# Distance-16 scores copied by ScalarE, and seven places for the raw operands of the down products

## The chip, the cores and the metric

The kernel runs on one core of one Trainium2 chip. The core has TensorE (PE, matmuls; its weight loads are shown as PEld), VectorE (DVE), ScalarE (ACT), GpSimd (POOL) and SyncE (SP), which here issues every DMA. The metric is the device time of one execution in microseconds, the median of three runs.

## What is computed

One step of a one-layer streaming encoder, on a prompt of 1024 frames and a running stream of 32 frames, all in float32, with D_MODEL 1024 and D_FF 2816:

```python
def run_trunk(x, states, params):          # DEPTH = 1
    ...
    h, st_new = mixer(rms_norm(x, g_mix_pre[l]), st, ...)
    x = x + rms_norm(h, g_mix_post[l])
    h, ffn_buf = conv_ffn(rms_norm(x, g_ffn_pre[l]), states[6][l], ...)
    x = x + rms_norm(h, g_ffn_post[l])

def conv_ffn(xn, buf, w_up, conv_w, conv_b, w_down):
    up = xn @ w_up
    up, buf = causal_dwconv(up, buf, conv_w, conv_b)
    gate, val = jnp.split(up, 2, axis=-1)
    return (jax.nn.gelu(gate, approximate=True) * val) @ w_down, buf

def gated_linear_scan(q, k, v, log_a, s0, L):     # in chunks of L = 64 (32 for the stream)
    def step(s, inp):
        ...
        diff = b[:, :, None] - b[:, None, :]
        decay = jnp.where(mask, jnp.exp(jnp.where(mask, diff, 0.0)), 0.0)
        scores = jnp.einsum('bihd,bjhd,bijhd->bijh', qc, kc, decay)
        o = (jnp.einsum('bijh,bjhv->bihv', scores, vc)
             + jnp.einsum('bihk,bhkv->bihv', qc * jnp.exp(b), s))
        ...
```

The mixer projects its input, runs three groups of heads (two gated linear scans of 6 and 5 heads, and 5 mLSTM heads), norms and gates them, and projects back.

## The kernel before

**Products in two halves.** Float32 operands are split into a rounded high half and the rest: ACT casts (line 95), DVE subtracts (line 98), and each product becomes three matmuls (lines 89 to 91).

**Units and levels.** Tokens are worked in units of 128 (u = 0 to 7, each two chunks of 64) and one of 32 (u = 8). Inside a chunk the decays between two positions are built by distance: `level` makes, for c = 32, 16, 8, 4, 2, 1, the scores between the first and the second half of every block of 2c positions, into a PSUM tile sc that has one buffer and takes two levels at a time. `copy_scores` places them in the score matrix P. The first level is copied by ACT as plain rectangles; all others go through `put`, a DVE copy under a mask (line 808). The mixers of one group of units run among the in-projections of the next.

**Up and down.** The up projection is computed in a Strassen form with seven products (tiles pux, puw, puy, puz) over 22 steps f. The down projection has two parts. The units 0, 8 and 4 take a plain product (tiles pd, into eight PSUM banks) over f, whose transposed rows of h are loaded into hr (two buffers of 288 columns). The other six units take seven products p1, p2, p6, p5, p3, p7, p4 (function `seven`), each a sum over k = 0 to 10. For one k, 384 columns of rows (h_d, or sums in s_d) and 512 columns of weights (w_dn, or sums in t_d) are loaded into one raw tile, here named rp, whose pool tag y0 has three buffers. `h_halves` makes hhp and hlp from the rows (two buffers each for odd and for even k), `weight_halves` makes wdp (seven buffers), and three PSUM banks (pdx, pdy or pdw) take three matmuls each. When a product is done, its banks are copied or added to others, and finished units are normed and stored. The tags y0 (3), y1 (1), st (1) and bw (2) are those of the up projection's results; down there only y0 is used again.

**Order.** The order of instructions on each engine is planned before compilation: `play` is a list scheduler over the whole program that keeps a queue for each engine, prices each instruction (`PRODUCT` for the matmuls by columns, a queue model for the DMAs) and takes the ready one with the longest tail. Every engine then works strictly in that order. A DMA's consumers become ready in the plan at `stop`.

Of the kernel before, what the change touches and what calls it, by code (L numbers as in the profile page):

```python
# [9 lines left out]
F32 = mybir.dt.float32  # L10
# [21 lines left out]
NCOL = 2 * HW  # L32
# [9 lines left out]
def fcol(u):  # L42

    return 128 * u if u < 4 else SMP if u == 8 else GAP_P + 2 + 128 * (u - 4)
# [35 lines left out]
def body(ctx: ExitStack, tc: tile.TileContext, a: dict):  # L80
    nc = tc.nc
    act, dve, pool, pe, sp = nc.scalar, nc.vector, nc.gpsimd, nc.tensor, nc.sync
# [588 lines left out]
    def mixer(u, g, ci0):  # L671
        n = 128 if u < 8 else DEC
# [130 lines left out]
        def put(c, src):  # L803
            mk_ = masks[:n, lev_index[c]:lev_index[c] + 1, :cl]
            dst = P[:n, :, :cl]
            if c:
                mk_, dst, src = second(mk_, c), second(dst, c), src.rearrange("p h (b c) -> p h b c", c=c)
            dve.copy_predicated(dst, mk_.broadcast_to([n, 11, *mk_.shape[2:]]), src)  # L808
# [39 lines left out]
        def copy_scores(c, sc, lv):  # L848
            s = sc[:, :, 32 * lv:32 * lv + cl // 2]
            if c == levels[0]:  # L850
                for (o, m) in chunks:
                    act.copy(P[o:o + c, :, c:2 * c], s[o:o + c])
            else:
                put(c, s[:n])

# [15 lines left out]
        for lv, c in enumerate(pairs[0]):  # L871
            copy_scores(c, sc, lv)
# [38 lines left out]
        for lv, c in enumerate(pairs[1]):  # L911
            copy_scores(c, sc, lv)
# [72 lines left out]
    P = mx.tile([128, 11, 64], F32, name="P")  # L985
# [319 lines left out]
    def down_all(ph, p6, gp):  # L1305
        xres = {}

        def wide(name):
            return p6.tile([128, 1024], F32, tag="wide", name=name, bufs=4)
# [33 lines left out]
        def h_halves(name, w, r, pool_, tag):  # L1343
            hh, hl = (pool_.tile([128, 384], F32R, tag=f"{tag}{x}", name=f"h{x}{name}", bufs=2) for x in "hl")
            split(hh[:, :w], hl[:, :w], r, dve)
            return hh, hl


        off, w = {}, 0
        for u in FIRST:  # L1350
            off[u] = w
# [2 lines left out]
        banks = [p.tile([128, 512], F32, tag=t, name=f"pd0_{i}", bufs=b) for i, (p, t, b) in enumerate(where)]  # L1354
        pair = []
        for f in range(NF):
            r = ph.tile([128, 288], F32, tag="hr", name=f"hr{f}", bufs=2)
            for u in FIRST:
                n = 128 if u < 8 else DEC
                sp.dma_start(r[:, off[u]:off[u] + n], h_d[f, :, fcol(u):fcol(u) + n])  # L1360
            hh, hl = h_halves(f"0_{f}", w, r, ph, "h")
            wr = praw[0].tile([128, 1024], F32, tag="raw", name=f"wd0_{f}r", bufs=2) if f < 2 else                 wide(f"wd0_{f}r")
            sp.dma_start(wr, a["w_dn"][f])
            wd = [weight_halves(f"wd0_{f}{hf}", wr[:, 512 * hf:512 * hf + 512]) for hf in range(2)]
            pair.append(wr)
            if f % 2:
                if f // 2 >= len(EARLY):
                    sums(f // 2, pair)
                pair = []
            if f == NF - 6:  # L1370
                sp.dma_start(gp, a["grows"][1:2, :].broadcast_to([128, 1024]))
                for u in FIRST:
                    residual(u)
            for d in range(8):
                c = slice(128 * (d % 4), 128 * (d % 4) + 128)
                mm3(banks[d][:, :w], [t[:, c] for t in wd[d // 4]], (hh[:, :w], hl[:, :w]), f == 0, f == NF - 1)
# [27 lines left out]
        def seven(p, ps, first):  # L1404
            ops = []
            for k in range(NP):
                r = ph.tile([128, NCOL], F32, tag="y0", name=f"r{p}_{k}", bufs=3)
                sp.dma_start(r[:, :384], ASRC[p](k))
                sp.dma_start(r[:, 384:896], BSRC[p](k))
                hh, hl = h_halves(f"{p}_{k}", 384, r[:, :384], *((ph, "h") if k % 2 else (p6, "g")))  # L1410
                wd = weight_halves(f"wd{p}_{k}", r[:, 384:896])
                ops.append((k, hh, hl, wd))
                if k == NP - 2:
                    continue
                for i in range(3):
                    c = slice(128 * i, 128 * i + 128)
                    for (j, hh, hl, wd) in ops:
                        mm3(ps[i], (hh[:, c], hl[:, c]), wd, first and j == 0, j == NP - 1, skip_group_check=True)
                ops = []
                if k % 3 == 0 and todo:  # L1420
                    todo.pop(0)()
# [173 lines left out]
AHEAD = {"mx": 10000., "psm": 10000., "pdx0": 1400., "pdx1": 700., "pdw0": 1400., "pdw1": 700., "pt": 130000.}  # L1595
ENGINES = ("PE", "DVE", "Activation", "Pool", "SP")
WINDOW = 3413.3
PRODUCT = {512: 232., 384: 175.5, 288: 133.5, 282: 131.5, 274: 126.5, 256: 118.}
PACKET = ((4, 9), (32, 9), (128, 13), (256, 18), (512, 27), (1024, 46), (1536, 65), (2048, 84), (4096, 159), (8192, 330), (1 << 16, 2640))
TABLES = {"Ln": 5, "Gelu_apprx_tanh": 11, "Exp": 0, "Tanh": 0, "Square": 0}  # L1600

# [94 lines left out]
def _product(i):  # L1696
# [9 lines left out]
    if mode == (128, 128) or (mode == (128, 32) and not f32) or mode == (32, 128):  # L1706
        g = PRODUCT.get(n, n / 2.4 + 12) if not f32 else max(n * 2 / 2.4 + 2.5, 60) if tr else 2 * max(n * 2 / 2.4 + 8, 112)
        return g, True, (128, 128) if mode == (128, 32) else mode, cells, (r, sums)
# [160 lines left out]
def play(g, tail, change, slack=None):  # L1869
# [6 lines left out]
    rows, held, seen, known, count = {}, [], [-1] * len(g.pred), dict.fromkeys(ENGINES, -1), 0  # L1876
    port, queue = {"DVE": 0., "Pool": 0.}, 0.
# [24 lines left out]
    while True:  # L1902
        t, e = min(((free[e] if ready[e] else max(free[e], at[wait[e][0][2]]), k) for k, e in enumerate(ENGINES) if ready[e] or wait[e]),
                   default=(None, None))
        if e is None:
            break
        e = ENGINES[e]
        while wait[e] and wait[e][0][0] <= t + 1e-6:
            heapq.heappush(ready[e], heapq.heappop(wait[e])[1:])
        if not ready[e]:  # L1910
            heapq.heappush(ready[e], heapq.heappop(wait[e])[1:])
        if e == "PE" and len(ready[e]) > 1:
            c = min(heapq.nsmallest(12, ready[e]), key=lambda x: x[0] + (change if mm[x[1]][2] != mode else 0))
            ready[e].remove(c)
            heapq.heapify(ready[e])
        else:
            c = heapq.heappop(ready[e])
        n = c[1]
        t = max(t, at[n])
        d, own, lock = cost[n]  # L1920
        sync = max([known[e]] + [seen[q] for q in g.pred[n] if eng[q] != "PE" or e != "PE"])
        if e == "PE" and any(k in rows and rows[k][0] != mm[n][4][0] and rows[k][1] > sync for k in mm[n][4][1]):
            held.append(c)
            continue
        if e == "SP" and queue - t - 1400 > BACKLOG:
            heapq.heappush(ready[e], c)
            free[e] = queue - 1400 - BACKLOG + 5
            continue
        if e == "Pool" and lock and port["DVE"] > t:
            heapq.heappush(ready[e], c)  # L1930
            free[e] = port["DVE"] + 5
            continue
        if e == "SP":
            free[e] = t + own
            queue = max(t + 1400, queue) + d
            stop = queue + 650
        elif e == "PE":
            d, wide, m, cl, (row, sums) = mm[n]
            if mode not in (None, m):
                t = max(t, max(cells) + (93 if mode == (128, 128) else 45))  # L1940
            mode, t = m, max([t] + [cells[c] for c in cl])
            if wide:
                free[e] = clock.run(t, d)
                cells = [free[e]] * 16
                stop = free[e] + 166
            else:
                f = clock.factor(t)
                for c in cl:
                    cells[c] = t + d * f
                clock.add(t, 14)  # L1950
                free[e] = t + 14 * f
                stop = t + d * f + 168
        else:
            if e == "DVE" and lock:
                t = max(t, port["Pool"])
                port["DVE"] = t + d
            if e == "Pool" and lock == 1:
                port["Pool"] = t + d
            if g.table[n] not in (None, table):
                table = g.table[n]  # L1960
                t += 1283
            free[e], stop = t + own, t + d
        if e == "PE":
            rows.update((k, (row, count)) for k in sums)
            seen[n], count = count, count + 1
            if sync > known[e]:
                while held:
                    heapq.heappush(ready[e], held.pop())
        else:
            seen[n] = sync  # L1970
        known[e] = sync
        start[n], end[n] = t, stop
        seq[e].append(n)
        release(n)
# [143 lines left out]
```

## Time and profile before

| | us |
|---|---|
| median of three runs (lowest to highest) | 1357.84 (1354.48 to 1359.75) |
| the profiled execution: time | 1356.24 |
| its span from the first to the last instruction | 1354.4 |
| PE busy in the span | 1303.9 |
| mean granted TensorE clock | 0.992 |

In the profile, a row of a stretch gives for each engine the busy time and, in brackets, the number of instructions, then the granted clock, the mean busy share of the 16 DMA engines and the GB/s moved. A timeline row gives the start, the duration, the engine, the line, the operation, the tiles written and read and the count; in square brackets stands how long the engine had been idle before it, and what ended that. A row of the waits gives the waiting engine and tile, what released it, the total, the times and the longest. Buffer numbers are left out of the names: wdp stands for wdp1 to wdp7, and so on.

### The profile page before, as it was taken

How to read it: one execution, taken by the hardware profiler on the slowest of the kernel's cores; microseconds unless marked ns; L12 is line 12 of the kernel's file. 1: busy time of each engine (PE TensorE's matmuls, PEld its weight loads, DVE VectorE, ACT ScalarE, POOL GpSimd, SP SyncE). 2: the span in 40 equal slices, each digit the busy share in tenths (PEclk: the TensorE clock that was granted, in tenths of full speed). 3: DMA queues.
4: the chain of work that ended last, by engine and by line, in shares of the span. 5: the costliest groups of instructions: out<-in, count | busy, mean ns of one | idle time of the engine just before them, and what ended most of it. 6: DMA issues, size and time to landing. Idle time of an engine off the chain costs nothing.

```text
span 1354.4 us, 30370 instructions
## 1 busy us (share of the span) xinstructions
PE 1303.9 (96%) x11977; PEld 1207.9 (89%) x11977; DVE 1039.2 (77%) x1884; ACT 710.6 (52%) x1400; POOL 181.9 (13%) x331
## 2 busy tenths in 40 slices
PE   6999999999999999999899999999999999998997
PEld 5999999998898887678899999999999999886775
DVE  6795549757889468878899988888888877755576
ACT  5654556545576554436754544545545454555554
POOL 2010100100102112222012211111111110000011
PEclk9999999999999999999999999999999999999998
DMA  9899869976898964635156623323223189786675
GB/s 327 260 330 332 266 243 333 301 260 203 287 305 288 331 231 121 202 95 171 69 199 230 215 97 109 102 87 119 80 87 119 71 275 290 261 265 192 218 248 205
DMA packets 148422, 285.24 MB, mean 211 GB/s; under 512 B 30039, under 2 KB 84471, under 8 KB 148279
## 3 DMA queue, kind: packets, MB, share of 16 engines
q1 hardware_dynamic: 148279, 283.30, 62.2%
q8 instruction: 94, 1.54, 0.5%
q14 instruction: 49, 0.40, 0.1%
HBM read 201.90 MB, written 81.34 MB: 209 GB/s over the span
## 4 chain that ended last, share of the span: by engine, by line
PE 69%; DMA 14%; DVE 9%; ACT 4%; issue 3%; SPq 1%; POOL 0%; DVEq 0%; ACTq 0%; POOLq 0%
PE pux L91 4%; PE pux L89 4%; PE pux L90 4%; PE pv L89 4%; PE pv L91 4%; PE pv L90 4%; DMA rp<-t_d 4%; PE pf L89 3%; PE pf L91 3%; PE pf L90 3%; PE puw L90 3%; PE puw L91 3%; PE puw L89 3%; DMA rp<-in_w_dn 2%; PE zp L89 2%
## 5 line engine op out<-in xcount | busy, mean ns | idle before, releaser
L1250 DVE SCALAR_TENSOR_TENSOR y<-uu,fconv_sb,y 128x1060 f32<-128x1060 f32 x88 | 115.8, 1320 | 7.9 <-ACT y L1248 7.4
L98 DVE TENSOR_TENSOR wdp<-rp,wdp 128x512 fp32r<-128x512 f32 x77 | 53.2, 691 | 56.2 <-ACT wdp L95 55.9
L95 ACT CAST wdp<-rp 128x512 fp32r<-128x512 f32 x77 | 47.7, 620 | 70.4 <-DMA rp<-t_d 39.0
L1248 ACT ACTIVATE y<-uu,fconv_sb 128x1060 f32<-128x1060 f32 x44 | 56.1, 1278 | 25.9 <-POOL uu L1245 21.5
L1196 ACT COPY c<-pux 128x274 f32<-128x274 f32 (+1 forms) x132 | 46.3, 381 | 33.9 <-PE pux L91 30.1
L926 POOL TENSOR_TENSOR hrs<-hss,mhalf 128x5 f32<-128x5 f32 (+3 forms) x27 | 35.8, 1330 | 175.3 <-DVE hss L925 172.6
L89 PE MATMUL pv<-wt_0h,xh 128*128 128x256 f32 (+2 forms) x195 | 53.8, 297 | 2.6 <-DVE xl L309 1.3
L91 PE MATMUL pv<-wt_0h,xl 128*128 128x256 f32 (+2 forms) x195 | 51.7, 288 | 0.0
L90 PE MATMUL pv<-wt_0l,xh 128*128 128x256 f32 (+2 forms) x195 | 51.5, 287 | 0.0
L89 PE MATMUL pdx<-wdp,hhp 128*128 128x512 f32 x132 | 44.8, 404 | 6.7 <-ACT hhp L95 4.6
L89 PE MATMUL pv<-wt_1h,xh 128*128 128x256 f32 (+2 forms) x195 | 49.1, 288 | 0.0
L91 PE MATMUL pv<-wt_1h,xl 128*128 128x256 f32 (+2 forms) x195 | 48.6, 288 | 0.0
L1245 POOL COPY uu<-fcache_sb 128x2 f32<-128x2 f32 x44 | 23.4, 531 | 186.1 <-DVE uu L1201 186.1
L90 PE MATMUL pv<-wt_1l,xh 128*128 128x256 f32 (+2 forms) x195 | 48.3, 288 | 0.0
L98 DVE TENSOR_TENSOR hlp<-rp,hhp 128x384 fp32r<-128x384 f32 x77 | 41.8, 552 | 5.4 <-ACT hhp L95 2.9
L90 PE MATMUL pdx<-wdp,hhp 128*128 128x512 f32 x132 | 43.9, 395 | 0.0
L91 PE MATMUL pdx<-wdp,hlp 128*128 128x512 f32 x132 | 42.9, 395 | 0.1
L95 ACT CAST hhp<-rp 128x384 fp32r<-128x384 f32 x77 | 38.4, 511 | 5.8 <-PE pdx L90 3.1
L89 PEld LDWEIGHTS pv<-wt_0h,xh 128*128 128x128 f32 (+1 forms) x195 | 35.2, 189 | 4.6 <-DVE xl L309 1.6
L211 POOL TENSOR_SCALAR gss<-gss 128x1 f32<-128x1 f32 (+1 forms) x9 | 7.4, 817 | 233.7 <-ACT gjk L1324 158.2
L89 PEld LDWEIGHTS pdx<-wdp,hhp 128*128 128x128 f32 x132 | 24.8, 191 | 13.9 <-ACT hhp L95 6.7
L808 DVE COPY_PREDICATED P<-masks_sb,sc 128x352 f32<-128x352 int32 (+1 forms) x44 | 29.8, 678 | 8.8 <-PE sc L773 8.3
(1781 smaller groups left out, 5144.4 us busy)
## 6 DMA issues: line engine op xcount, KB each, us to landing
h_d<-y SPq DMA_DIRECT2D x22, 530.0 KB, 5.1
rp<-t_d SPq DMA_DIRECT2D x44, 256.0 KB, 3.8
wt_0r<-in_w_tok SPq DMA_DIRECT2D x21, 512.0 KB, 5.9
wt_1r<-in_w_tok SPq DMA_DIRECT2D x21, 512.0 KB, 5.0
rp<-in_w_dn SPq DMA_DIRECT2D x33, 256.0 KB, 3.7
rp<-s_d SPq DMA_DIRECT2D x44, 192.0 KB, 3.9
wt_0l<-lt_d SPq DMA_DIRECT2D x14, 512.0 KB, 4.7
wt_1l<-lt_d SPq DMA_DIRECT2D x14, 512.0 KB, 5.8
```

The lines of the kernel that those rows point to most:

```text
L89: pe.matmul(ps, lh[0], rh[0], start=first, stop=False, **kw)
L90: pe.matmul(ps, lh[0], rh[1], start=False, stop=False, **kw)
L91: return pe.matmul(ps, lh[1], rh[0], start=False, stop=last, **kw)
L95: act.copy(hi, src)
L98: (eng or pool).tensor_tensor(lo, src, hi.bitcast(F32), op=ALU.subtract)
L211: pool.tensor_scalar(out, ss, other, EPS, op0=ALU.add, op1=ALU.add)
L808: dve.copy_predicated(dst, mk_.broadcast_to([n, 11, *mk_.shape[2:]]), src)
L926: pool.tensor_tensor(rs[:n, h0:h0 + nh], ss[:n, h0:h0 + nh], mhalf[:n, :nh], op=ALU.pow)
L1196: act.copy(t, ps)
L1245: pool.tensor_copy(u[:, GAP_S:GAP_S + 2], fcache[:, j, :])
L1248: act.activation(y, u, AF.Identity, scale=fconv[:, j, 2:3], bias=fconv[:, j, 3:4])
L1250: dve.scalar_tensor_tensor(y, uu[i][:, s:s + NCOL], fconv[:, j, s:s + 1], y, op0=ALU.mult, op1=ALU.add)
```

## The change

Three edits. The level c = 16 is copied by ACT as four rectangles of 16 partitions by 11 heads by 16 columns; in the unit of 32 that level is the first one and was copied so before. The raw tiles of the seven products rotate over seven places of the same size in the tags y0, bw, y1 and st, and every second pair of hr tiles takes a bw buffer. And numbers of the planner change: the prices of matmuls, and a load counts as landed 1250 instead of 650 ns after its packets.

```diff
             if c == levels[0]:
                 for (o, m) in chunks:
                     act.copy(P[o:o + c, :, c:2 * c], s[o:o + c])
+            elif c == 16:
+                for o in range(0, n, 32):
+                    b = o % 64
+                    act.copy(P[o:o + c, :, b + c:b + 2 * c], s[o:o + c, :, b // 2:b // 2 + c])
             else:
                 put(c, s[:n])
...
+        places = [("y0", 3), ("bw", 2), ("y0", 3), ("y1", 1), ("y0", 3), ("bw", 2), ("st", 1)]
+        count = [0]
+
+        def raw(name):
+            t, b = places[count[0] % 7]
+            count[0] += 1
+            return ph.tile([128, 896], F32, tag=t, name=name, bufs=b)
...
-            r = ph.tile([128, 288], F32, tag="hr", name=f"hr{f}", bufs=2)
+            r = ph.tile([128, 288], F32, tag="hr", name=f"hr{f}", bufs=2) if f % 4 < 2 else \
+                ph.tile([128, 288], F32, tag="bw", name=f"hr{f}", bufs=2)
...
-                r = ph.tile([128, NCOL], F32, tag="y0", name=f"r{p}_{k}", bufs=3)
+                r = raw(f"r{p}_{k}")
...
-PRODUCT = {512: 232., 384: 175.5, 288: 133.5, 282: 131.5, 274: 126.5, 256: 118.}
+PRODUCT = {512: 227.5, 384: 175., 288: 132.5, 282: 131., 274: 127., 256: 119.5}
...
         if e == "SP":
             free[e] = t + own
             queue = max(t + 1400, queue) + d
-            stop = queue + 650
+            stop = queue + 1250
```

The new numbers move instructions nearly everywhere. In the rows below, the number behind a name's k tells one tile from another.

On ACT, at the start of the product p6 before (wdp_k and hhp_k are the halves of weights and rows of step k, rp_k their raw tile):

```order
L95 CAST wdp_0_15923<-rp_0_15916 128x512
L95 CAST hhp_10_15888<-rp_10_15885 128x384
L95 CAST wdp_1_15942<-rp_1_15935 128x512
L95 CAST hhp_1_15938<-rp_1_15935 128x384
L95 CAST hhp_0_15919<-rp_0_15916 128x384
L95 CAST wdp_2_15961<-rp_2_15954 128x512
L95 CAST wdp_3_15980<-rp_3_15973 128x512
L95 CAST hhp_2_15957<-rp_2_15954 128x384
L95 CAST hhp_3_15976<-rp_3_15973 128x384
```

The casts of weights and of rows of one k follow each other closely.

At the same place now:

```order
L95 CAST wdp_0_15947<-rp_0_15940 128x512
L95 CAST hhp_9_15902<-rp_9_15899 128x384
L95 CAST wdp_1_15966<-rp_1_15959 128x512
L95 CAST hhp_10_15912<-rp_10_15909 128x384
L95 CAST wdp_2_15985<-rp_2_15978 128x512
L95 CAST hhp_1_15962<-rp_1_15959 128x384
L95 CAST wdp_3_16004<-rp_3_15997 128x512
L95 CAST hhp_0_15943<-rp_0_15940 128x384
L95 CAST wdp_4_16023<-rp_4_16016 128x512
L95 CAST hhp_3_16000<-rp_3_15997 128x384
L95 CAST wdp_5_16042<-rp_5_16035 128x512
```

The casts of weights now stand two to three k ahead of those of the rows.

On SP, in the first down product (hr are its rows, wd its weights, t_d the stored sums), p1's raw tiles before:

```order
L1236 DMA t_d<-wd_20r 128x1024
L1409 DMA rp_3_15495<-in_w_dn 128x512
L1408 DMA rp_3_15495<-h_d 128x384
L1236 DMA t_d<-wd_21r 128x1024
L1409 DMA rp_4_15537<-in_w_dn 128x512
L1408 DMA rp_4_15537<-h_d 128x384
```

The loads of k = 3 and 4 stand behind the last stores of the weights' sums.

Now they stand among the hr loads:

```order
L1422 DMA rp_2_15500<-in_w_dn 128x512
L1373 DMA hr_15028<-h_d 128x128 x2
L1373 DMA hr_15028<-h_d 128x32
L1376 DMA wd_15r<-in_w_dn 128x1024
L1421 DMA rp_2_15500<-h_d 128x384
L1422 DMA rp_4_15561<-in_w_dn 128x512
L1373 DMA hr_15074<-h_d 128x128 x2
L1373 DMA hr_15074<-h_d 128x32
L1421 DMA rp_4_15561<-h_d 128x384
L1240 DMA t_d<-wd_12r 128x1024
```

Four of them (k = 2, 3, 4 and 6) are issued before the first of those stores or soon behind it; k = 1 and 5 wait for the bw places behind the hr loads.

On ACT, at the scores of the third unit now (vth are gates, wt weights of the in-projection):

```order
L852 COPY P<-sc_0_2544 32x11x32 x2
L856 COPY P<-sc_0_2544 16x11x16
L324 CAST wt_7_0h<-wt_7_0r 128x1024
L101 ACTIVATE vth_5_4008<-pv_5_3982 128x256
L856 COPY P<-sc_0_2544 16x11x16 x2
L101 ACTIVATE vth_5_4038<-pv_5_4012 128x256
L856 COPY P<-sc_0_2544 16x11x16
```

The four new copies (line 856) stand partly behind other work of ACT; before, one masked copy stood on DVE in their place.

## The prediction

> **What bounds the kernel now.** I read the busy shares first, then the same engines in six stretches cut where the work changes, then the list of waits, and then the timeline at the places where TensorE stands still.
>
> ```profile
> PE 1303.9 (96%) x11977; PEld 1207.9 (89%) x11977; DVE 1039.2 (77%) x1884; ACT 710.6 (52%) x1400; POOL 181.9 (13%) x331
> ...
> core 0: us, PE busy (x) PEld busy (x) DVE busy (x) ACT busy (x) POOL busy (x), PEclk, DMA share, GB/s
> 0.00:200.00 200.00, 185.88 (x1471) 175.89 (x1472) 124.40 (x222) 108.88 (x194) 20.83 (x47) 1.00 0.87 296
> 200.00:640.00 440.00, 428.48 (x5599) 378.78 (x5597) 343.12 (x776) 235.89 (x522) 68.43 (x88) 0.99 0.72 239
> 640.00:1110.00 470.00, 464.56 (x3752) 462.66 (x3752) 407.23 (x609) 242.43 (x435) 79.26 (x180) 1.00 0.38 132
> 1110.00:1171.00 61.00, 58.74 (x436) 57.36 (x435) 48.82 (x83) 29.13 (x57) 0.00 (x0) 1.00 0.90 293
> 1171.00:1347.00 176.00, 166.25 (x726) 133.19 (x724) 111.89 (x192) 93.73 (x194) 11.36 (x15) 0.99 0.69 224
> ```
>
> TensorE (PE) is the bound nearly everywhere, so a change can only bring what PE waits. The idle time is stretch minus busy: 14.1 us in the first 200, 11.5 in the mixer stretch, 5.4 in the up stretch, 2.3 where the first down product runs, and 9.8 in the seven down products. The last is dense for its length (5.5% against 2.6% in the mixers), and there PE should have nothing but products. I take it apart next: these are the seven products' casts and subtracts, and who waits for what.
>
> ```profile
> L95 ACT CAST hhp<-rp x77: 494/511/526, 1110.3 to 1341.1; 128x384 fp32r<-128x384 f32 x77
> L98 DVE TENSOR_TENSOR hlp<-rp,hhp x77: 535/552/559, 1114.6 to 1341.8; 128x384 fp32r<-128x384 f32 x77
> L95 ACT CAST wdp<-rp x77: 605/621/625, 1165.1 to 1337.7; 128x512 fp32r<-128x512 f32 x77
> L98 DVE TENSOR_TENSOR wdp<-rp,wdp x77: 673/692/694, 1165.8 to 1338.3; 128x512 fp32r<-128x512 f32 x77
> ...
> DMA to landing us min/median/max: 2.9/4.0/5.6
> ...
> ACT wdp L95 <- DMA rp<-t_d: 39.0, 33, 2.1
> ACT wdp L95 <- DMA rp<-in_w_dn: 30.8, 23, 2.9
> ```
>
> The two wait rows (releaser, us in total, times, the longest) say that 56 of the 77 weight casts found their raw operand not landed and ScalarE (ACT) stood 69.8 us for it. A wait of ACT costs nothing by itself; the next rows show where it reaches PE.
>
> ```profile
> 1201.36 0.84 PE L89 MATMUL pdy<-wdp,hhp 128*128 128x512 f32 x3
> 1202.04 0.84 PE L90 MATMUL pdy<-wdp,hhp 128*128 128x512 f32 x3
> ...
> 1216.31 0.32 SPq L1409 DMA_DIRECT2D rp<-t_d  x1
> 1219.49 0.62 ACT L95 CAST wdp<-rp 128x512 fp32r<-128x512 f32 x1 [1.23 <-DMA rp<-t_d]
> 1220.75 1.02 DVE L98 TENSOR_TENSOR hlp<-rp,hhp 128x384 fp32r<-128x384 f32 x2
> 1221.33 0.32 SPq L1409 DMA_DIRECT2D rp<-t_d  x1
> 1224.64 0.62 ACT L95 CAST wdp<-rp 128x512 fp32r<-128x512 f32 x1 [1.80 <-DMA rp<-t_d]
> 1225.73 0.50 PE L89 MATMUL pdx<-wdp,hhp 128*128 128x512 f32 x1 [2.02 <-ACT hhp L95]
> ...
> 1251.61 0.74 PE L89 MATMUL pdw<-wdp,hhp 128*128 128x512 f32 x2 [1.71 <-ACT hhp L95]
> ...
> 1299.27 0.98 PE L89 MATMUL pdx<-wdp,hhp 128*128 128x512 f32 x3 [1.79 <-ACT hhp L95]
> ...
> 1319.63 0.62 ACT L95 CAST wdp<-rp 128x512 fp32r<-128x512 f32 x1 [2.12 <-DMA rp<-t_d]
> ...
> 1322.18 0.47 PE L89 MATMUL pdx<-wdp,hhp 128*128 128x512 f32 x1 [2.12 <-DVE cl L1454]
> ```
>
> Three products start 0.68 us apart (1201.36 to 1202.04), so one takes 0.227 us and the nine of one k take 2.04. A place of the raw operand goes round in 5.02 us: its load is issued at 1216.31, its cast begins at 1219.49, the last subtract that reads it ends at 1220.75 + 0.55, and the next load is issued at 1221.33. With three places that is 1.67 us per k, only 0.37 under PE's 2.04. A landing of 5.6 instead of the 3.2 seen here makes it 7.4 / 3 = 2.47, over PE's. So the loop cannot get ahead, and whatever ACT and VectorE (DVE) do besides at the turn from one product to the next is paid by PE. That is where the four rows with 2.02, 1.71, 1.79 and 2.12 us stand. In the last of them the sums of DVE are named, but behind a cast that had waited 2.12 us for its load.
>
> **The change, part by part.** *Seven places (the main term).* The loads keep their number, size and queue; what changes is how early a load can be issued. Seven places make 5.02 / 7 = 0.72 us per k, and 7.4 / 7 = 1.06 with the late landing, both far below 2.04. Next come ACT with 0.62 + 0.51 = 1.13 and DVE with 0.69 + 0.55 = 1.24 us per k, both under 2.04 too. The planned order shows the use of it: the casts of the weights run two to three k ahead of those of the rows. How much PE loses now:
>
> ```profile
> L89 PE MATMUL pdx<-wdp,hhp x132: 387/389/628, 1171.7 to 1345.9; 128*128 128x512 f32 x132
> ...
> L89 PE MATMUL pdw<-wdp,hhp 128*128 128x512 f32 x66 | 21.7, 395 | 2.5 <-ACT hhp L95 1.7 <-ACT cl L1445 0.8
> ...
> L89 PE MATMUL pdy<-wdp,hhp 128*128 128x512 f32 x33 | 9.5, 396 | 0.2 <-ACT hhp L95 0.2
> ...
> L1389 PE MATMUL ptsx<-ident,accd 128*128 128x128 f32 (+1 forms) x12 | 1.8, 273 | 0.0
> ```
>
> Each of lines L89 to L91 has 132 + 66 + 33 products, 693 in all, so 157.3 us. The stretch from 1171.7 to about 1346.6 is 174.9 long; with 3.6 for the two groups of 12 transposes, 14.0 us are lost. That is more than the 9.8 counted idle, because the first product after a stop counts as busy for 0.4 to 0.5. I let 3.0 remain: 0.8 for the ACT copies of the bank at 1271 (in the pdw row), and some 2 in product p7, where DVE becomes the late one: 11 x 1.24 = 13.6 for the halves, and at most 3 x (0.68 + 2 x 0.69 + 2 x 0.73) = 10.6 for the sums and the ends of three units, 24.2 against the 22.4 of PE. So -11.0 us, with 0 and -14.0 as ends.
>
> [...]
>
> *Four buffers for the rows of the first product instead of two.* They borrow the two bw places.
>
> ```profile
> ACT hh L95 <- DMA hr<-h_d: 9.0, 8, 2.7
> ...
> PE pd L89 <- ACT hh L95: 2.2, 5, 0.7
> ...
> 1129.00:1165.00 36.00, 33.76 (x248) 32.61 (x248) 27.88 (x48) 15.69 (x31) 0.00 (x0) 1.00 0.92 301
> ```
>
> PE loses 2.2 us to them, but the DMA engines are 92% busy, so an earlier issue does little: -0.5, ends 0 and -2.2. The cost is that p1's loads of k = 1 and 5 want the same places and are issued after the hr loads; the casts of k = 1 are due only when the eight banks of the first product are done, and the other five places hold k = 0, 2, 3, 4, 6 by then.
>
> *Scores of distance 16.* Eight units (the short one has 16 as its first level and copies already) each lose one masked copy on DVE and get four small copies on ACT.
>
> ```profile
> L852 ACT COPY P<-sc x17: 295/444/448, 164.8 to 571.7; 32x352 f32<-32x352 f32 x16, 16x176 f32<-16x176 f32 x1
> ...
> 246.73 0.56 DVE L808 COPY_PREDICATED P<-masks_sb,sc 128x352 f32<-128x352 int32 x1
> ```
>
> The single 16x176 copy took 0.295 us, so ACT gets 32 x 0.295 = 9.4 us and DVE loses 8 x 0.56 = 4.5. ACT is busy 235.9 of 440 us in the mixer stretch and takes 2% more; DVE falls from 78% to 77%. The score banks (sc, one buffer) are held by 2 x 0.444 + 4 x 0.295 = 2.07 us of ACT instead of 0.89 beside DVE's 0.56, 1.2 us longer per unit, with PE's in-projections in front of the next scores. I cost it at 0; if that cover were gone, 8 x 1.2 = 9.4 us.
>
> *The planner's numbers.* Product prices move by at most 2%, and a load counts as landed 0.6 us later; this deals the whole order anew, DMA queue included. For a 256 KB load the plan's landing goes from 1.40 + 0.77 + 0.65 = 2.8 us to 3.4, and the measured median is 4.0, so it moves towards the trace. What new stalls or savings it makes outside the down stage no row shows. Bounds: of the 31.1 us idle before 1110 the 8 of the start stay, so at best -23; at worst as much again, +23. I take 0, since the rows nearest to it are single stops such as these, of about 2 us, which a new order moves about rather than removes.
>
> ```profile
> PE xt L306 <- DVE x L295: 8.0, 1, 8.0
> ...
> PE mi L585 <- ACT dcs L581: 2.0, 1, 2.0
> ```
>
> **Sum.** The profiled execution took 1356.24 us (span 1354.4 and 1.84 around it), 1.6 under the median of the runs, 1357.84. -11.0 - 0.5 + 0 + 0 = -11.5 gives 1344.7 for it, and 1346.3 against the median, which is my number.
>
> **Rivals.**
> - *The next late thing takes half back.* With loads early, the turns from product to product stay: DVE's 24.2 us in p7's 22.4, and copies that free a bank. If half of the 11.0 stays, 1346.3 + 5.5 = 1351.8. For it: DVE is busy 21.06 of 25 us there already, 84% (row below). Against it: in the up stretch DVE is busy 87% and PE loses 1.2%.
>
> ```profile
> 1297.00:1322.00 25.00, 21.27 (x92) 16.55 (x90) 21.06 (x36) 14.05 (x31) 5.15 (x6) 1.00 0.85 280
> ...
> rp<-t_d SPq DMA_DIRECT2D x44, 256.0 KB, 3.8
> ...
> rp<-s_d SPq DMA_DIRECT2D x44, 192.0 KB, 3.9
> ```
>
> - *Transfers set the pace, the change does nothing.* If more loads in flight land later in proportion, the rate stays, and the time is 1357.8. For it: 0.90 of the DMA engines at 293 GB/s just before. Against it: the products need 256 + 192 KB, 0.459 MB, per 2.04 us, so 225 GB/s, and the stretch moved 224 at a share of 0.69.
> - *The score copies come onto the path:* 1346.3 + 9.4 = 1355.7. Against it: no row has PE waiting for the copies of L852. [...]
> - *Slower: the new order stalls the mixers.* Engines take their work in order, so one piece put before a later load holds all behind it. It decides from 11.5 + 6.8 = 18.3 us of new idle, the mixer stretch's 11.5 going to 29.8: two stops of 1 us more for each of nine units. With 20, 1366. Against it: the plan's landing comes closer to the measured one.
> [...]
>
> **How the numbers follow.** Chances: forecast 0.62, half back 0.16, no effect 0.09, score copies 0.05, slower 0.06, faster products 0.02. 0.5% of 1357.84 is 6.8 us, about what a measurement here tells from no change; so faster means below 1351.0. The forecast is that but for an edge of 0.02, the half-back case in 0.03 of its 0.16, the last case wholly: 0.65. Same is the rest of these with no effect and the copies: 0.29; slower 0.06. The forecast's own range is 1341 to 1351; to leave out no more than 2 in 10 the range has to take in half back and the copies: 1340 to 1356.
>
> **What would show it.** Right: ACT's wait for rp falls from 69.8 us to under 15, the seven products are 162 to 166 us long instead of 174.9, and no PE stop of 1.7 us and more behind a cast is left there; line L808 has 45 copies instead of 53 with no new PE wait for P or sc. Wrong: landings of rp above 5.6 us in the median, PE waiting for DVE's sums at the turns, or idle in the first 640 us off its 25.6 by more than 5.

## The result, and the profile after

The changed kernel took 1336.83 us (median of four runs, 1336.63 to 1340.31); the kernel before, run beside it, 1358.80. The ratio is 0.9865, with a 95% interval of 0.9835 to 0.9896. So it is faster, by some 18 us going by the ratio (the two medians lie 22.0 apart) where 11.5 were forecast, and the median lies 3.2 us under the low end of the range.

The profiled execution of the changed kernel took 1340.31 us, 15.9 less than that of before. First its busy shares, then the stretches that answer to the five of before, cut where its own stages change (start, mixers, up, first down product, seven products):

```profile
PE 1299.9 (97%) x11977; PEld 1209.8 (90%) x11977; DVE 1034.1 (77%) x1876; ACT 724.3 (54%) x1432; POOL 184.3 (14%) x331
```

```profile
0.00:200.00 200.00, 187.73 (x1373) 177.16 (x1374) 124.09 (x217) 111.60 (x200) 19.85 (x47) 0.99 0.86 296
200.00:635.00 435.00, 424.92 (x5697) 375.98 (x5695) 337.85 (x773) 244.63 (x547) 69.70 (x85) 0.99 0.74 241
635.00:1102.00 467.00, 460.28 (x3706) 458.69 (x3705) 402.60 (x604) 238.58 (x428) 81.69 (x182) 0.99 0.37 130
1102.00:1170.00 68.00, 66.14 (x481) 65.00 (x480) 53.35 (x91) 33.98 (x65) 0.00 (x0) 0.97 0.92 306
1170.00:1331.00 161.00, 160.88 (x727) 132.98 (x725) 112.18 (x189) 94.86 (x193) 11.65 (x16) 1.00 0.71 235
```

In the last stretch PE is busy 160.88 of 161.00 us. From the first of the seven products to the last they take 162.3 us, 175.0 before: 12.7 of the 15.9 us. Another 5.0 came ahead of the up projection, which starts at 628.87 instead of 633.87, and 1.9 were given back between the two: from the start of the up projection to the first of the seven products it takes 539.7 us instead of 537.8. The groups of the casts and the list of waits say why the seven are dense:

```profile
L95 ACT CAST hhp<-rp 128x384 fp32r<-128x384 f32 x77 | 39.6, 515 | 50.4 <-PE pdx L90 19.0
...
L95 ACT CAST wdp<-rp 128x512 fp32r<-128x512 f32 x77 | 47.2, 620 | 10.2 <-PE pdx L91 3.3
```

```profile
ACT hhp L95 <- DMA rp<-s_d: 4.4, 6, 0.7
```

The weights' casts wait for loads 1.4 us in all, the rows' casts 4.7, of which this row has 4.4; before, ACT stood 69.8 us for loads. Now it stands for PE to free the halves' buffers, which is the order of things wanted: PE is what everything waits for. And the products themselves have no idle time in front of them:

```profile
L89 PE MATMUL pdx<-wdp,hhp 128*128 128x512 f32 x132 | 43.1, 393 | 0.0
...
L89 PE MATMUL pdw<-wdp,hhp 128*128 128x512 f32 x66 | 20.3, 389 | 0.0
...
L89 PE MATMUL pdy<-wdp,hhp 128*128 128x512 f32 x33 | 9.6, 389 | 0.0
```

### The profile page after: what moved, and what is told of

It reads as the page before. It is cut to its first block, busy times and chain, and to the rows that moved or that the text cites. A ratio compares the mean times of both kernels' runs of the same rounds, so it can differ in the third digit from the quotient of the medians.

```text
span 1338.5 us, 30466 instructions
## 1 busy us (share of the span) xinstructions
PE 1299.9 (97%) x11977; PEld 1209.8 (90%) x11977; DVE 1034.1 (77%) x1876; ACT 724.3 (54%) x1432; POOL 184.3 (14%) x331
## 4 chain that ended last, share of the span: by engine, by line
PE 83%; DMA 5%; DVE 5%; ACT 3%; issue 2%; POOL 1%; SPq 1%; DVEq 0%; ACTq 0%; POOLq 0%
PE pux L89 4%; PE pv L89 4%; PE pux L91 4%; PE pux L90 4%; PE pv L91 4%; PE pv L90 4%; PE pf L89 4%; PE pf L91 4%; PE pf L90 4%; PE puw L90 3%; PE puw L89 3%; PE puw L91 3%; PE pdx L89 2%; PE pdx L90 2%; PE pdx L91 2%; PE sc L773 2%
## 5 line engine op out<-in xcount | busy, mean ns | idle before, releaser
L98 DVE TENSOR_TENSOR hlp<-rp,hhp 128x384 fp32r<-128x384 f32 x77 | 42.6, 556 | 39.3 <-ACT hhp L95 11.5
L1249 POOL COPY uu<-fcache_sb 128x2 f32<-128x2 f32 x44 | 27.5, 624 | 188.5 <-DVE uu L1205 188.5
L91 PEld LDWEIGHTS pv<-wt_0h,xl 128*128 128x128 f32 (+1 forms) x195 | 34.4, 189 | 1.1 <-issue 0.6
L89 PEld LDWEIGHTS pv<-wt_1h,xh 128*128 128x128 f32 (+1 forms) x195 | 33.5, 189 | 1.6 <-ACT xh L308 1.5
```

What stands on the lines that cost most here:

```text
L89: pe.matmul(ps, lh[0], rh[0], start=first, stop=False, **kw)
L91: return pe.matmul(ps, lh[1], rh[0], start=False, stop=last, **kw)
L98: (eng or pool).tensor_tensor(lo, src, hi.bitcast(F32), op=ALU.subtract)
L1249: pool.tensor_copy(u[:, GAP_S:GAP_S + 2], fcache[:, j, :])
```

## Experiments

Two ways to read the times are used. Ratios are to the kernel before, run in turn with it on the same chip, with 95% intervals. The times of one kernel also follow the granted clock of the run: a fit over all 154 runs, with a level for each kernel in each series of runs and one slope, gives 1.02 (± 0.09) us for each 0.001 of clock. "At equal clock" below means those levels at 0.992, less that of before in the same series. The standard error of each such difference is 0.8 to 1.2 us, and some 1.5 us where two of them from different series are compared. "The seven" is the time from the first to the last of the seven products in the profile, "mixers" the time until the up projection starts. A single profile tells the mixers only roughly: five kernels whose planned order of PE is the same up to there took 628.4 to 635.4 us.

Three theories stood at the outset. A: the raw places carry the gain. B: the planner's numbers do as much. C: the score copies make the mixers faster. Each edit was first made alone.

**The seven places alone.**

```diff
+        places = [("y0", 3), ("bw", 2), ("y0", 3), ("y1", 1), ("y0", 3), ("bw", 2), ("st", 1)]
...
-                r = ph.tile([128, NCOL], F32, tag="y0", name=f"r{p}_{k}", bufs=3)
+                r = raw(f"r{p}_{k}")
```

> Kernel before with the seven raw places alone: hr keeps two buffers, the scores their masked copy, the planner its old numbers. The planned order is that of before up to the up projection, so nothing can change ahead of it. Theory A (a place goes round in 5.0 us, so three places are too few): the down stage gives what it gave in the changed kernel, 10 to 12 us off, 1346 to 1348; ACT's wait for rp under 15 us; no PE stop over 1.5 us behind a cast. Theory B (the planner's numbers do it, also in the down stage, by putting ACT's and DVE's other work where loads really land): the places alone give at most 4 us, 1354 or more.

Ratio 0.9923 (0.9892 to 0.9955), 11.8 us at equal clock. The seven took 162.7 us. The planned order of PE up to the up projection is that of before, so this gain lies in the down stage. A holds in full.

**The planner's numbers alone.**

```diff
-PRODUCT = {512: 232., 384: 175.5, 288: 133.5, 282: 131.5, 274: 126.5, 256: 118.}
+PRODUCT = {512: 227.5, 384: 175., 288: 132.5, 282: 131., 274: 127., 256: 119.5}
...
-            stop = queue + 650
+            stop = queue + 1250
```

> Kernel before with the planner's new numbers alone (prices of matmuls, landing 1250). Theory A: the first pux product starts some 5 us earlier as in the changed kernel, the seven products keep their loss of about 14 us, so 1352 to 1354, 4 to 6 us off. Theory B: the down stage gains as well, 1340 to 1346. Theory C (the 5 us ahead of the up projection come from the score copies): nothing, 1356 to 1360.

Ratio 0.9949 (0.993 to 0.9969), 5.4 us at equal clock. The number is inside A's 4 to 6, but not for A's reason: the seven took 167.5 us with the three old places instead of keeping their loss, while the mixers became longer, 639.6 us. So a better order removes more than half of the time that the places remove there, and these two gains cannot add in full.

**The score copies alone.**

```diff
+            elif c == 16:
+                for o in range(0, n, 32):
+                    b = o % 64
+                    act.copy(P[o:o + c, :, b + c:b + 2 * c], s[o:o + c, :, b // 2:b // 2 + c])
```

> Kernel before with the four ACT copies of the scores of distance 16 alone. Theory A (they are hidden, cost and gain 0): 1355 to 1360, with the order dealt anew from the first mixer on, which may move single stops by 1 to 3 us. Theory C (a shorter DVE queue is what speeds the mixers): 3 to 6 us off, 1352 to 1355, the first pux product some 5 us earlier. Were the copies on the path: 9 us more, 1367.

Ratio 0.9949 (0.9923 to 0.9974), 5.1 us at equal clock. The seven stayed as they were (174.4); the mixers took 627.0 us. My price of 0 was wrong, and C was right that they pay.

**Four raw places under the old numbers.**

```diff
+        places = [("y0", 3), ("y0", 3), ("y0", 3), ("y1", 1)]
```

> Kernel before with four raw places instead of three (the fourth in the y1 tag). Theory A: 5.02 / 4 = 1.26 us per k, and 7.4 / 4 = 1.85 with the latest landing, both under PE's 2.04, so four places should already bring most of it: 8 to 11 us off, 1347 to 1350. If the lead itself is what counts (work at the turns of ACT and DVE to be bridged), four places bring a third to a half of the seven places' gain, 1352 to 1355. Theory B: 0 to 2 us.

Ratio 1.0017 (0.9993 to 1.004), 0.5 us slower at equal clock: no gain. Of the cases expected only the smallest, B's, holds, and not for B's reason. The seven took 174.2 us. The timeline of this kernel at the start of p6 shows where the fourth place went (I name the steps from the planned order: the first row is the weights' cast of step 2, the load is that of step 4, then come the weights and rows of step 3, the weights of step 4, and last the rows of step 2, for which PE waits):

```profile
1213.85 0.62 ACT L95 CAST wdp<-rp 128x512 fp32r<-128x512 f32 x1
...
1216.54 0.43 SPq L1417 DMA_DIRECT2D rp<-t_d  x1
...
1217.76 0.62 ACT L95 CAST wdp<-rp 128x512 fp32r<-128x512 f32 x1 [2.45 <-DMA rp<-t_d]
1218.29 0.51 ACT L95 CAST hhp<-rp 128x384 fp32r<-128x384 f32 x1
1220.74 0.62 ACT L95 CAST wdp<-rp 128x512 fp32r<-128x512 f32 x1 [1.94 <-DMA rp<-t_d]
1221.26 0.51 ACT L95 CAST hhp<-rp 128x384 fp32r<-128x384 f32 x1
...
1221.82 0.97 PE L89 MATMUL pdx<-wdp,hhp 128*128 128x512 f32 x3 [3.52 <-ACT hhp L95]
```

The tile of step 2 had its weights cast at 1213.85, yet its rows are cast only at 1221.26. The planner had put the weights of steps 3 and 4 ahead of them, and these casts stood 2.45 and 1.94 us for loads. ACT ran the casts in the planned order, so PE waited 3.52 us for rows behind another step's load. And the tile's place was held meanwhile. Over the six products after p1 a place is held 6.7 us in the mean with three places, 8.9 with four: 2.23 and 2.22 us per k, so the place bought nothing.

This gave a theory of room (L below): the number of places times PE's 2.04 us, less the time by which the rows' cast follows the weights' cast, less 1.3 for the last reads, is what is left for a landing. The rival (N) is that the number of places alone decides. Two kernels tell them apart.

**Four places with all the rest of the change.**

```diff
-        places = [("y0", 3), ("bw", 2), ("y0", 3), ("y1", 1), ("y0", 3), ("bw", 2), ("st", 1)]
+        places = [("y0", 3), ("y0", 3), ("y0", 3), ("y1", 1)]
```

> The changed kernel with four raw places instead of seven; score copies, hr buffers and planner's numbers stay. Theory L (what counts is the room left for a landing: places x 2.04 us, less the stretch from the weights' cast to the rows' cast, less 1.3 us for the last reads): the rows' cast stands 2.5 casts behind the weights' cast here, 3.2 in the four places under the old numbers, so 8.16 - 2.55 - 1.3 = 4.3 us are left for a landing, against 3.6 there and a median landing of 4.0: seven products of 164 to 168 us, 1338 to 1344 us in all. Theory N (the number of places alone decides, as four under the old numbers gained nothing): 171 to 175 us for the seven, 1346 to 1351 in all.

Ratio 0.9861 (0.9838 to 0.9884), as good as the change with seven. The seven took 161.6 us, under the 164 to 168 that L expected. The loads are still waited for, but nearly always in front of ACT only; PE has one stop of over 0.25 us left. Two rows of the waits in the seven products, the landing times, the stretch of the seven and the stop:

```profile
ACT wdp L95 <- DMA rp<-t_d: 26.4, 26, 3.2
ACT wdp L95 <- DMA rp<-in_w_dn: 15.8, 15, 2.4
```

```profile
DMA to landing us min/median/max: 2.7/4.1/6.6
```

```profile
1164.60:1326.20 161.60, 160.63 (x721) 132.26 (x719) 110.97 (x189) 93.21 (x192) 7.77 (x16) 1.00 0.75 243
```

```profile
1303.41 0.47 PE L89 MATMUL pdx<-wdp,hhp 128*128 128x512 f32 x1 [0.92 <-DVE cl L1467]
```

**Five places under the old numbers.**

```diff
+        places = [("y0", 3), ("bw", 2), ("y0", 3), ("bw", 2), ("y0", 3)]
```

> The kernel before with five raw places (tags y0 and bw), nothing else. Theory L: the rows' cast stands 4.4 casts behind the weights' cast, 5 x 2.04 - 4.47 - 1.3 = 4.4 us are left for a landing, as in the four places under the new numbers: seven products of 164 to 168 us, 6 to 10 us off the time before. Theory N with a threshold between four and seven: either 162 to 163 us as with seven places (10 to 12 us off) or 173 to 175 as with four (0 to 2 off). The first arithmetic of the prediction, 5.02 / 5 = 1.0 us per k, gives the full 10 to 12 us off.

Ratio 0.9918 (0.9895 to 0.994), 11.7 us at equal clock; the seven took 162.4 us, the full gain. N is refuted by the two kernels with four places. L ordered the kernels rightly but expected 164 to 168 us in both of its tests, a gradual return; what came is nearer to a threshold:

| kernel | places | rows' cast after weights' cast, us, median | held, us, mean | room for a landing, us | the seven, us |
|---|---|---|---|---|---|
| before | 3 | 0.94 | 6.68 | 3.2 | 175.0 |
| new prices alone | 3 | 0.94 | 6.52 | 3.2 | 169.7 |
| four, old numbers | 4 | 3.24 | 8.89 | 3.6 | 174.2 |
| planner's numbers alone | 3 | 0.58 | 6.38 | 3.7 | 167.5 |
| four, new numbers | 4 | 2.21 | 8.17 | 4.3 | 161.6 |
| five, old numbers | 5 | 4.99 | 10.31 | 4.4 | 162.4 |
| seven alone | 7 | 5.44 | 14.41 | 8.1 | 162.7 |

(The two columns in the middle are over the six products after p1. Room as in the expectations, from the mean distance of the two casts in the planned order, 1.02 us for each cast between.) Landings take 4.0 us in the median before, and 3.7 to 4.1 in four of the others: with less room than that PE stops at the turns, with more a single stop of 0.7 to 1.0 us is left. That the gap lies between 3.7 and 4.3 is what seven kernels show; below it the room does not order the lengths exactly. No kernel changed the room and left the rest of the order as it was, so that the room is the cause is argued, not shown.

**The change once more, and without the score copies.**

> The changed kernel once more, beside the kernel before on the same chip. Every reading expects 1336 to 1341 us, a ratio of 0.985 to 0.989, and seven products of 162 to 163 us. Its runs should differ by the granted clock: about 1.3 us for each 0.001 of it, since a half-clock window of 3.41 us follows a stop of PE and costs up to 1.7 us. Under the rival that the spread comes from the DMA, runs of equal clock differ by more than 4 us.

Ratio 0.9865 (0.9841 to 0.9888), 16.0 us at equal clock, the seven 162.6 us: the result repeats. Its runs went from 1332.63 at a clock of 0.997 to 1341.06 at 0.990, 1.2 us per 0.001, and those of one clock differ by 2.3 us at most. So the DMA is not needed for its spread; in the runs of before it isn't excluded (see the section on the clock).

> The changed kernel without the score copies of ScalarE: distance 16 goes by the masked VectorE copy again, places, hr buffers and the planner's numbers stay. Theory C (the copies make the mixers faster by themselves, some 5 us as when made alone): 4 to 6 us slower than the changed kernel, 1341 to 1344. Rival, the price of 0 in the prediction (alone they only dealt the order of the mixers anew, to a luckier one): within 2.5 us of the changed kernel, either side.

Ratio 0.9935 (0.9913 to 0.9957), 9.7 us at equal clock: 6.3 less than with the copies. The mixers took 638.4 us against 629.0. The edit is the one above, undone. The waits of PE for DVE in the mixers that differ most, first without the copies, then of the changed kernel:

```profile
PE og L773 <- DVE P L808: 3.6, 3, 2.9
...
PE pb L435 <- DVE vg L412: 2.4, 2, 2.0
```

```profile
PE pb L435 <- DVE vg L412: 0.7, 2, 0.4
...
PE og L773 <- DVE P L808: 0.4, 1, 0.4
```

The first row looks like the masked copy on the path, but it isn't the one that the change removes. Its longest wait, without the copies, is this:

```profile
502.01 0.48 DVE L924 TENSOR_TENSOR cat<-hn,gt 32x320 f32<-32x320 f32 x1 [5.82 <-DMA gt<-g_d]
...
503.01 0.52 DVE L808 COPY_PREDICATED P<-masks_sb,sc 32x176 f32<-32x176 int32 x1
503.63 0.53 DVE L808 COPY_PREDICATED P<-masks_sb,mi 32x352 f32<-32x352 int32 x1
...
504.21 1.04 PE L773 MATMUL og<-v,P 32*32 32x64 f32 x12 [2.91 <-DVE P L808]
```

Both copies have 32 partitions: they belong to the unit of 32, whose copies the change leaves alone, and they stood behind another instruction of DVE that had waited 5.82 us for a load. The 5.1 us that the copies bring under the old numbers are not in these waits either: there they were 0.3 and 0.5 us before the copies, and nothing and 0.8 with them. So the gain of the copies is measured, but no wait of PE is shown that goes with the removed copies.

**Places and copies together, old numbers; the change with the old landing.**

```diff
-PRODUCT = {512: 227.5, 384: 175., 288: 132.5, 282: 131., 274: 127., 256: 119.5}
+PRODUCT = {512: 232., 384: 175.5, 288: 133.5, 282: 131.5, 274: 126.5, 256: 118.}
...
-            stop = queue + 1250
+            stop = queue + 650
```

This is the first one's edit against the changed kernel; the hr tiles have two buffers again as well.

> The seven places and the score copies, with the planner's old numbers and two hr buffers. If the two parts add (alone 12 and 5 us at equal clock): 16 to 18 us off, 1337 to 1339; mixers of 626 to 629 us as with the copies alone, seven products of 162 to 163.5. If the planner's new numbers are needed beside them: 4 us or more slower than the changed kernel, 1340 and above.

Ratio 0.9905 (0.9884 to 0.9926), 14.1 us at equal clock; mixers 629.1, the seven 162.6. That is between the two cases expected. Beside the places the copies bring 2.3 us at equal clock, and the planner's numbers with the hr buffers the last 1.9. Both are differences between series, good to some 1.5 us: neither is told clearly from nothing, nor the 2.3 from the 5.1 that the copies brought alone.

The second one's edit against the changed kernel:

```diff
-            stop = queue + 1250
+            stop = queue + 650
```

> The changed kernel with a load again counted as landed 650 ns after its packets; the new prices of the matmuls, the copies, the places stay. With seven places the plan's landing should not matter: seven products of 162 to 163 us, and mixers of 626 to 630 us if the copies make them faster in any order, so 1335 to 1340. If the mixers of the changed kernel are good by a lucky order only, this third order with the copies should fall anywhere in 628 to 640 us: 1337 to 1349.

Ratio 0.9913 (0.9893 to 0.9934), 12.5 us at equal clock; the seven 161.9 as expected. The mixers took 632.2, the longest of the orders with copies: outside the 626 to 630 expected if the copies help in any order, and inside the 628 to 640 of the lucky order.

**The new prices alone; the hr buffers alone.**

```diff
-PRODUCT = {512: 232., 384: 175.5, 288: 133.5, 282: 131.5, 274: 126.5, 256: 118.}
+PRODUCT = {512: 227.5, 384: 175., 288: 132.5, 282: 131., 274: 127., 256: 119.5}
```

> The kernel before with the new prices of the matmuls alone. It splits the planner's numbers: if the later landing made the down products faster (167.5 us with both numbers), they are back at 173 to 176 us here; if the prices did, 166 to 169. The mixers get a third order without the copies: 628 to 640 us, as the two others span. In all 1350 to 1360.

Ratio 1.0038 (1.0022 to 1.0055): slower, 2.7 us at equal clock. The seven got shorter (169.7), which lies between the two cases expected, but the mixers took 640.5. By difference the later landing is worth 8.1 us beside the new prices (5.4 + 2.7).

```diff
-            r = ph.tile([128, 288], F32, tag="hr", name=f"hr{f}", bufs=2)
+            r = ph.tile([128, 288], F32, tag="hr", name=f"hr{f}", bufs=2) if f % 4 < 2 else \
+                ph.tile([128, 288], F32, tag="bw", name=f"hr{f}", bufs=2)
```

> The kernel before with four buffers for the rows of the first down product, nothing else. The prediction gave it 0.5 us, between 0 and 2.2: a ratio of 0.998 to 1.002. In the trace the first down product's PE waits for the rows' casts, 2.2 us before, should fall below 1. Rival: the bw buffers come free later than the hr ones, and nothing changes there.

Ratio 0.9989 (0.9972 to 1.0006), 1.6 us at equal clock: inside the 0 to 2.2 forecast, and by the ratio not told from nothing. PE's wait for the rows' casts fell from 2.2 to 0.7 us, and 1.1 of waiting for DVE's half came instead.

The mixers ran in three orders without the copies (mean 632.2 us over five profiles, 639.0 over two, 640.5) and in three with them (628.1 over two, 628.7 over three, 632.2). The copies are ahead under each set of numbers: 4.1 us with the old, 10.3 with the new, and 8.3 where only the prices are new. The first is less than the 7.0 by which profiles of one order differ. In none is it all idle time of PE: with the old numbers 1.7 of the 4.1 us are (25.3 us idle in the mean without the copies, 23.6 with them). Another part is the clock: of the steps at half clock (see the section on the clock), the two profiles with the new numbers and no copies hold six and five, the three with copies three, four and one.

## Why the prediction was right or wrong

**Seven places: right, and the arithmetic behind it was not.** Of the 14.0 us lost, 11.0 were to come back and 3.0 to stay. In the profile 12.7 came, and 162.3 - 157.3 - 3.6 = 1.4 stayed; alone the places gave 11.8 at equal clock. ACT's wait fell under 15, the seven lie inside 162 to 166, and no stop over 0.25 us is left there. The p7 term (DVE 24.2 us in PE's 22.4) did not come about. But the cycle of 5.02 us that I divided by the places was a short one: the mean is 6.68, so three places turned over once in 2.23 us, and not 1.67. (Not even 2.23 says what sets the pace. It contains the stops of PE itself, and with seven places the same division gives 14.41 / 7 = 2.06, PE's own pace.) And dividing by the number is not the rule: with four places the planner holds each longer, and by 5.02 / 4 = 1.26 the four should have given everything. I quoted the order that does it (weights' casts ahead of the rows') as the use of the change, without asking what a weights' cast that waits does to the rows behind it.

**Score copies: the step that failed.** Their term stood in the sum at 0. The count was right: 32 copies of 0.296 us on ACT, 8 masked copies fewer on DVE, as the groups of the mixers show.

```profile
L808 DVE COPY_PREDICATED P<-masks_sb,sc 128x352 f32<-128x352 int32 (+1 forms) x36 | 25.5, 708 | 6.0 <-PE sc L773 5.4 <-ACT wf_10h L324 0.2
L856 ACT COPY P<-sc 16x176 f32<-16x176 f32 x32 | 9.5, 296 | 0.5
```

The price was 0 with a loss of 9.4 as the only end, since I looked for what ACT's extra work would delay. The gain end was missing: 4.5 us less on an engine that is busy 78% of the stage and for which PE waits. They brought 5.1 us alone, 6.3 beside everything else and 2.3 beside the places. Whether it is DVE's shorter queue or the order that the planner makes of it is not separated and stays open. That it holds in three pairs of orders speaks for the first; that the largest wait that went with them is one behind a load, and that a third order with the copies took 632.2 us, no less than the mean without them under the old numbers, speaks for the second.

**Planner's numbers: the size was off, the sign open.** I had 0 within ±23. Alone they gave 5.4 us, as a gain in the seven products and a loss in the mixers. Beside the places and the copies they and the hr buffers are worth 1.9 at equal clock, which is hardly told from nothing. That a new order moves stops about rather than removes them fits the mixers, and failed for the seven products.

**hr buffers: right** within what can be told, -0.5 forecast.

**The sum.** At equal clock the steps from before to the change are 11.8 (places), 2.3 (copies), 1.9 (numbers and hr): 16.0, against 11.5; only the first of them is well above its error. The rest of the measured 18 us is the clock: runs of before had 0.992 in the mean, those of the change 0.9945 to 0.9948, which the slope of 1.02 us for each 0.001 makes some 2.5 to 3 us.

**The rivals.** None of the signs of being wrong came: landings of rp have a median of 3.7 us, PE waits for DVE's sums at no turn, and its idle time ahead of the up projection is 22.4 us instead of 25.6. The next late thing took nothing back. The transfers did not set the pace: the seven moved 235 GB/s at a share of 0.71, above the 225 they need. The copies did not come onto the path. The new order did stall the mixers, as the slower rival has it, but only without the copies (up to 640.5 us). Products did not move closer: 157.3 us of products at 0.227 leave 1.4 of the 162.3, and no run shows the closer spacing that has 0.02 of the chances.

## What the runs showed of the clock

A stop of PE cost more than itself here. The rows below are four steps of 3.4 us of the kernel before, at the stop of 2.12 us that the prediction quotes (the columns as above; PEclk is the third from the end):

```profile
1316.40:1319.80 3.40, 3.40 (x15) 2.50 (x14) 1.56 (x3) 0.79 (x3) 0.00 (x0) 1.00 0.98 339
1319.80:1323.20 3.40, 1.28 (x7) 0.86 (x6) 2.88 (x5) 1.93 (x5) 0.00 (x0) 0.99 1.11 399
1323.20:1326.60 3.40, 3.40 (x10) 2.63 (x8) 3.37 (x7) 2.94 (x9) 0.00 (x0) 0.50 0.99 383
1326.60:1330.00 3.40, 3.40 (x16) 2.82 (x15) 1.99 (x4) 1.30 (x3) 0.00 (x0) 1.00 0.91 308
```

In the second step PE is busy 1.28 us; in the third it is busy throughout at a granted clock of 0.50 and does 10 products where 15 or 16 are usual: 5 to 6 products, 1.1 to 1.4 us, on top of the 2.12. In the 14 profiles of this study there are 63 such stretches at 0.50, 58 of 3.41 us and 5 of twice that, besides one at the end of each. In the profile of before they begin 350.36, 449.35, 551.75, 657.56 and 1323.16 us into the span, in that of the changed kernel at 158.86, 421.68, 476.30, 643.55, 653.79 and 1165.79: those of one profile lie whole multiples of 3.413 us apart, on one grid. In the grid step that holds the stop of 2.12 us PE was busy for 0.38 of the step. Of the grid steps of all 14 profiles between 24 and 1330 us in which PE was busy for less than 0.45 of the step, 29 of 32 were followed by such a stretch; between 0.45 and 0.55, 21 of 38; between 0.55 and 0.75, 8 of 87; above that 5 stretches began behind some 5200 steps. The profiles of before and of the changed kernel have 3 of 3, 5 of 8, 2 of 13 and 1 of 740 of these. So by these counts what a stop cost here went mostly by how much of it fell into one step. Where the grid lies differs from profile to profile: counted from the start of the span, its steps begin at 2.20 us before and at 1.84 in the changed kernel. The same order has one to three such stretches in its mixers. This is a part of why runs of one kernel differ, by up to 14.6 us: the slope on the clock takes about half of the variance between them, and two runs of the kernel before at the same granted clock of 0.993 still lie 10.9 us apart (1348.44 and 1359.33). What makes the other half stays open. That a kernel with fewer stops gains a little more than their sum in this way is my estimate from the 1.1 to 1.4 us above; no run shows it.

## What to carry to other kernels

Count the buffers of a load not by its round trip alone but by what holds them: a tile that two readers share is held until the later reader comes, and a scheduler with one more buffer may only hold each longer, as here 8.9 us with four places and 6.7 with three. Then look at what stands behind a waiting instruction in the order of its engine: here casts of steps further on, which stood 2.45 and 1.94 us for their loads, delayed the step that was due, and PE waited 3.52 us for it. Price work taken off a busy engine on both sides, and look at what a wait stands behind before it is put down to the work taken off. Do not count a stop of TensorE by its length alone: with what followed, the 2.12 us above cost 3.2 to 3.5.
